# Both partition halves for the low part of the attention keys, and dearer products in the planner's prices

## The chip, the cores and the metric

The kernel runs on one core of a Trainium2 chip. The metric is device time in microseconds (us); three runs of the kernel before gave 3691.1, 3691.89 and 3694.82 us, median 3691.89. A profile of one execution, taken by the hardware profiler, stands beside them. Its engines are called PE (TensorE, matrix products), PEld (TensorE's loads of the stationary operand), DVE (VectorE), ACT (ScalarE), POOL (GpSimd, which here mostly issues transfers) and SP (SyncE, which issues the weight transfers).

## What is computed

Two transformer blocks, of two layers each, on 512 tokens of width 1024, with everything in float32. The parts that this change touches are the attention scores. The first block has neighbourhood attention and context attention in layer 0 (8 heads of 64), and grouped attention over 512 own and 256 context keys in layer 1 (16 query heads, 4 key heads of 64). Each layer of the second block mixes three kinds: latent attention (6 heads of 96), sliding-window attention (6 query heads, 2 key heads of 64) and stick-breaking attention (4 heads of 64).

```
# first block, layer 0 (8 heads, d = 64)
s_loc = einsum(q_r, k_r) * scale          # 256 keys of the window
s_ctx = einsum(q_r, k_ctx) * scale        # 256 context keys
# first block, layer 1 (16 heads on 4 key heads)
s = einsum(qg, k) * dh ** -0.5            # 512 + 256 keys
# second block, per layer
s = einsum(qb, kb) * D ** -0.5            # sliding window, up to 256 keys
z = einsum(qi, k) * scale                 # stick breaking, up to 512 keys, causal
```

Softmax (or the stick-breaking product) and the product with the values follow each; around them stand projections, gated feed-forward layers (width 2816) and norms.

## The kernel before

**Precision.** A float32 operand is split into a high and a low part, each of a type that TensorE takes in one pass. A dense product is then three products into one PSUM bank: high by high, high by low, low by high (`mm3`). Names end in `h` and `l`: `wh`, `wl` for weights, `hnh`, `hnl` for activations.

**Scores of heads of 64.** Here the split is stacked along the contraction. A query tile Q has 128 partitions: the high part of the head in one half of 64, the low part in the other. The key tile K holds the scaled high part of the keys in both halves, so one product of 128 rows gives (high query + low query) by high key. A second product adds high query by low key. The low part of the keys lies only in one half (64 partitions) of its tile (Kl; Klc for context keys, SKl in the second block), so this second product takes the 64 matching partitions of Q as its stationary operand: `q[hs]` by `Kl[hs]`, and a trace shows it as `64*128`, 64 rows by 128 columns. It is called the narrow product, or low product, below. The products of 128 rows show as `128*128`; the latent heads of the second block use three products of 96 rows (`S<-mqkh`, ...). The products with the values, `O<-PTs,...`, are `128*64`, and some of the modulation products `128*32`.

**Making the keys.** `kstack` (line 1560) has two phases. ACT writes the scaled high part to one half of K; then DVE writes the low part to its half of Kl, and ACT copies the high part to K's other half. In layer 0 both heads of a pair share one Kl and one Klc tile. In layer 1 (`g_keys`, line 2025) a pair of key heads shares one Kl, and all four share one Klc. In the second block (`k_item`, line 2416) a pair of stick-breaking heads shares one SKl, while the two sliding-window key heads have one each already (`g_swin`, line 2506).

**Attention pipeline.** `g_pipe` (line 1605) runs items in flight: scores (`qk`, lines 1635, 2080, 2850, 2938) and softmax of one item, transposes of the probabilities two items behind (PT in PSUM, copied by ACT to PTs), products with the values three behind (O). In layer 1 an item is a tile of 128 queries and a head: S<-K,Q and S<-Kl,Q of 512 columns, then Sc<-Kc,Q and Sc<-Klc,Q of 256. Projections of other heads or of the next part fill TensorE in between.

**What sets the order.** The code records its instructions first. A planner (`order`, line 379) then lists them: each engine takes the ready instruction of best priority, with prices in nanoseconds from `price` (line 340), forwards and backwards in four rounds. Tiles come from pools of fixed size: 56 slots of 128x512 (`g`), 8 PSUM banks (`b`), and some for weights. The result is one fixed order for each engine; at run time an engine takes its instructions in that order and waits for what they need. A product of the split type is priced by its columns alone: `max(columns / 2.4, 107) + 2.5`, 215.8 ns for 512 columns. Rows have no price, and a change of shape has none. `warm` (line 571) puts products of a constant with itself (`...<-cons 128x128`) into gaps of 500 ns or more that the plan has on TensorE.

All instructions are written out from one line, L628, so they are told apart by the tiles' names.

Of the kernel before, what the change touches and what calls it, by code (L numbers as in the profile page):

```python
# [165 lines left out]
class _View:  # L166
    """part of a tile; the steps to it are repeated on the real tile"""
# [37 lines left out]
    def box(self):  # L205
        """partitions and columns that bound the view"""
# [34 lines left out]
class _Program:  # L241
    """records instructions, orders them, writes them out"""
# [30 lines left out]
    # ---- recording  # L273
    def glue(self):
        """what is recorded next on one engine stays together"""
        self.glued = _Op()
        o = self.glued
        o.calls, o.pre, o.post, o.tiles, o.cost, o.lag, o.table = [], {}, [], [], 0.0, 0.0, None
# [61 lines left out]
    def price(self, o, name, args, kw, psum):  # L340
        """nanoseconds that an instruction holds its engine"""
        views = [v for v in args if isinstance(v, _View)]
        n = max(v.free() for v in views) if views else 0
        if o.eng == "tensor":
# [10 lines left out]
            else:  # L355
                o.cost += max(b.free() / 2.4, 107.0) + 2.5
# [17 lines left out]
    # ---- ordering  # L374
# [4 lines left out]
    def order(self, prio, seq, window=6000, patience=0.0, margin=0.0, backlog=1e9):  # L379
        """list scheduling: each engine takes the ready instruction of best priority.  # L380

        A tile is only taken if the instructions left can still be run in the order in which
        they stand in seq, with the slots that there are.
        """
# [11 lines left out]
        for t, a in live.items():  # L396
            assert a.max() <= self.caps[t], (t, int(a.max()), int(a.argmax()))
        done = bytearray(N + 1)
# [3 lines left out]
        parked = {t: [] for t in self.caps}  # L402
# [4 lines left out]
        push, pop = heapq.heappush, heapq.heappop  # L407

# [9 lines left out]
        while len(out) < N:  # L418
# [28 lines left out]
            # slots  # L447
            ok = True
            need = {}
            for x in o.tiles:  # L450
# [3 lines left out]
                if a > first and live[x.tag][first:a].max() >= self.caps[x.tag]:  # L454
                    parked[x.tag].append(o)
# [4 lines left out]
                if k > len(s):  # L460
                    parked[x.tag].append(o)
# [9 lines left out]
            for x in o.tiles:  # L471
                if not x.alloc:
# [3 lines left out]
                    if a > first:  # L476
                        live[x.tag][first:a] += 1
            cost = o.cost
# [10 lines left out]
            for x in o.tiles:  # L489
                x.end = max(x.end, o.end)  # L490
                l = x.left
                if len(l) == 1:
                    l.pop()
                    live[x.tag][first:o.k + 1] -= 1
                    push(slots[x.tag], (x.end + 250.0, x.slot))
                else:
# [5 lines left out]
                if parked[x.tag]:  # L502
                    for q in parked[x.tag]:
                        push(avail[q.eng], (q.prio, q.k))
                    parked[x.tag] = []
# [5 lines left out]
            if o.k == first:  # L511
# [5 lines left out]
                for tg in parked:  # L517
                    for q in parked[tg]:
                        push(avail[q.eng], (q.prio, q.k))
                    parked[tg] = []  # L520
# [3 lines left out]
    def mirror(self):  # L524
        """the program from its end to its start"""
# [22 lines left out]
    def schedule(self, rounds=4):  # L548
        """forwards and backwards in turn: what starts late in one direction is urgent in the other"""
# [21 lines left out]
    def warm(self, a, share=0.6, least=500.0):  # L571
        """products of a with itself where the tensor engine would wait: its clock halves when it idles.

        They write to a bank before the tile that comes next in it is started.
        """
# [38 lines left out]
    # ---- writing  # L614
# [16 lines left out]
class _Weights:  # L631
    """stream of weight units: loads run ahead, each unit is split exactly into two float32r parts"""
# [10 lines left out]
    def add(self, key, ap, nk, cols=256, tok=False, g=False):  # L643
        """a unit of nk contraction tiles, in parts: of columns, or (tok) of contraction tiles"""
# [19 lines left out]
    def phases(self, i):  # L664
        """the split of unit i in phases, each to be emitted some time after the one before"""
# [49 lines left out]
    def ahead(self):  # L715
        """the split of the unit after the next, once the matmuls of the present one are out"""
# [7 lines left out]
class _K:  # L724
# [55 lines left out]
    def run_bg(self, budget):  # L780
        """emit background work of about this many microseconds on the vector engine"""
# [20 lines left out]
    def g_rsqrt(self, v, n, out):  # L802
        """v ** -0.5 in small steps that depend on one another; out takes the result"""
# [22 lines left out]
    def sums(self, nt, parts):  # L826
        """sums over the partitions, token-major, of parts that are added one by one"""
# [10 lines left out]
    def stat_p(self, acc):  # L838
        """sums over the partitions, token-major"""
# [6 lines left out]
    def g_stat(self, p, n, out):  # L846
        """one over the root of the mean, from sums of squares"""
# [7 lines left out]
    def stat_b(self, r):  # L855
        """token-major column to a row on all partitions"""
# [6 lines left out]
    def g_row(self, acc, n):  # L863
        """the norm's row, step by step, in a slot of its own"""
# [23 lines left out]
    def apply_items(self, X, rb, A, B, his, los, sl):  # L888
        """scaled and shifted tiles of the normed stream, in two parts"""
# [17 lines left out]
    def update_items(self, X, o, rb, G, acc2, sl, add=None):  # L907
        """residual plus gated, normed branch; squares for the next norm"""
# [42 lines left out]
    def g_postpre(self, X, o, n, acc, G, A, B, his, los, step=256):  # L951
        """post-norm of a branch, residual, pre-norm of the next; one step of tokens after the other"""
# [135 lines left out]
    def load_row(self, i):  # L1088
        """one conditioning vector on all partitions, in two tiles"""
# [9 lines left out]
    def mod_tasks(self, key, rows, outs, bias, blocks):  # L1099
        """background products of conditioning vectors with columns of a modulation matrix"""  # L1100
# [20 lines left out]
    def mods_first(self, q, A, Ac):  # L1121
        """shift and scale of two tiles of features in layer 0, for both streams, on the tensor engine"""
# [25 lines left out]
    def g_mods0(self, r):  # L1148
        """2048 columns of layer 0's modulation for both streams on the tensor engine"""
# [64 lines left out]
    def g_proj_f(self, key, streams, post, step=1.2, k0=0):  # L1214
        """feature-major: weights stationary; post gives the phases after a group"""
# [21 lines left out]
    def g_proj_t(self, key, streams, post, step=1.2):  # L1237
        """token-major: activations stationary"""
# [1938 lines left out]
```

## Time and profile before

| what | before |
|---|---|
| device time, three runs | 3691.1, 3691.89, 3694.82 us |
| span of the profiled execution | 3693.1 us, 1.2 above the median run |
| PE busy | 3667.9 us (99%), 21332 products |
| DVE busy | 2421.1 us (66%) |
| ACT busy | 1601.6 us (43%) |
| POOL busy | 273.0 us (7%) |
| mean granted TensorE clock | 0.988 of full |

The span is the time from the first to the last instruction on the core. The products of a stream overlap, so the end of each is modelled and a busy PE says little about its speed; the distance from one start to the next says how long a product really holds the engine. A chain row follows the last instruction back to whatever released each step.

In order of time the span has: first block layer 0 with its attention (about 100 to 330 us) and two feed-forward layers, layer 1 with its attention (about 1000 to 1260), a feed-forward layer, and the second block's two layers, whose attention lies at about 2100 to 2300 and 3100 to 3310.

### The profile page before, as it was taken

How to read it: one execution, taken by the hardware profiler on the slowest of the kernel's cores; microseconds unless marked ns; L12 is line 12 of the kernel's file. 1: busy time of each engine (PE TensorE's matmuls, PEld its weight loads, DVE VectorE, ACT ScalarE, POOL GpSimd, SP SyncE). 2: the span in 40 equal slices, each digit the busy share in tenths (PEclk: the TensorE clock that was granted, in tenths of full speed). 3: DMA queues.
4: the chain of work that ended last, by engine and by line, in shares of the span. 5: the costliest groups of instructions: out<-in, count | busy, mean ns of one | idle time of the engine just before them, and what ended most of it. 6: DMA issues, size and time to landing. Idle time of an engine off the chain costs nothing.

```text
span 3693.1 us, 55815 instructions
## 1 busy us (share of the span) xinstructions
PE 3667.9 (99%) x21332; PEld 3078.3 (83%) x21332; DVE 2421.1 (66%) x5741; ACT 1601.6 (43%) x2985; POOL 273.0 (7%) x511
## 2 busy tenths in 40 slices
PE   9999999999999999999999999999999999999999
PEld 7689988899976888889888978888888889788887
DVE  4456845699977899998833569994453336694332
ACT  3554533365677643333222458322332235673221
POOL 0110000100001224000000000340000000000000
PEclk9999999999999999998999989999999999899999
DMA  9423322445322558322422322693322232122221
GB/s 319 156 78 132 114 92 97 136 160 184 126 83 101 189 186 288 112 86 76 151 94 84 92 64 90 239 337 103 99 84 97 94 96 77 34 65 97 92 97 63
DMA packets 142908, 458.51 MB, mean 124 GB/s; under 512 B 19872, under 2 KB 21936, under 8 KB 142640
## 3 DMA queue, kind: packets, MB, share of 16 engines
q1 hardware_dynamic: 104400, 331.54, 27.4%
q0 software_dynamic: 38240, 123.41, 9.8%
q8 instruction: 167, 2.74, 0.3%
q14 instruction: 101, 0.83, 0.1%
HBM read 445.43 MB, written 7.34 MB: 123 GB/s over the span
## 4 chain that ended last, share of the span: by engine, by line
PE 97%; DVE 1%; ACT 1%; DMA 0%; issue 0%; SPq 0%; ACTq 0%; DVEq 0%
PE U L628 45%; PE mm L628 32%; PE S L628 5%; PE tl L628 5%; PE O L628 3%; PE PT L628 3%; PE st L628 1%; PE v L628 1%; PE Sc L628 1%; PE mod L628 1%; PE tp L628 1%; PE R L628 0%; PE pq L628 0%; PE rb L628 0%; PE pkv L628 0%
## 5 line engine op out<-in xcount | busy, mean ns | idle before, releaser
L628 ACT ACTIVATE wh<-ws 128x1024 fp32r<-128x1024 f32 (+2 forms) x558 | 571.5, 1027 | 952.5 <-PE mm L628 455.0
L628 DVE TENSOR_TENSOR wl<-ws,wh 128x1024 fp32r<-128x1024 f32 (+2 forms) x558 | 659.9, 1185 | 400.4 <-ACT wh L628 394.9
L628 PE MATMUL U<-hnh,wh 128*128 128x512 f32 (+1 forms) x2048 | 792.5, 387 | 0.0
L628 PE MATMUL U<-hnl,wh 128*128 128x512 f32 (+1 forms) x2048 | 792.3, 387 | 0.0
L628 PE MATMUL U<-hnh,wl 128*128 128x512 f32 (+1 forms) x2048 | 792.0, 387 | 0.0
L628 PEld LDWEIGHTS U<-hnh,wl 128*128 128x128 f32 x2048 | 384.6, 188 | 84.5
L628 PEld LDWEIGHTS U<-hnl,wh 128*128 128x128 f32 x2048 | 384.6, 188 | 84.5 <-DVE hnl L628 0.2
L628 PEld LDWEIGHTS U<-hnh,wh 128*128 128x128 f32 x2048 | 384.5, 188 | 84.4
L628 PE MATMUL mm<-hdh,wl 128*128 128x512 f32 x960 | 378.3, 394 | 0.0
L628 PE MATMUL mm<-hdh,wh 128*128 128x512 f32 x960 | 378.2, 394 | 0.0
L628 PE MATMUL mm<-hdl,wh 128*128 128x512 f32 x960 | 377.9, 394 | 0.0
L628 DVE SCALAR_TENSOR_TENSOR wm<-wm,crow 128x512 f32<-128x512 f32 x384 | 249.8, 687 | 0.1
L628 DVE SCALAR_TENSOR_TENSOR cv<-U,vecs,cv 128x511 f32<-128x511 f32 (+1 forms) x264 | 173.2, 659 | 85.6 <-ACT cv L628 81.6
L628 PEld LDWEIGHTS mm<-hdl,wh 128*128 128x128 f32 x960 | 180.3, 188 | 42.4
L628 PEld LDWEIGHTS mm<-hdh,wl 128*128 128x128 f32 x960 | 180.2, 188 | 42.3
L628 PEld LDWEIGHTS mm<-hdh,wh 128*128 128x128 f32 x960 | 180.3, 188 | 42.0
L628 DVE TENSOR_TENSOR sg<-sg,U 128x512 f32<-128x512 f32 x88 | 60.6, 688 | 204.6 <-PE U L628 195.0
L628 ACT ACTIVATE cv<-U,vecs 128x512 f32<-128x512 f32 (+1 forms) x132 | 93.0, 706 | 224.0 <-PE U L628 224.0
L628 POOL DMA_DIRECT2D wm<-in_w_mod x288 | 154.3, 537 | 330.2 <-DVE wm L628 88.4
L628 PE MATMUL mm<-wh,hnh 128*128 128x256 f32 (+1 forms) x576 | 169.3, 294 | 0.0
L628 ACT ACTIVATE sg<-U 128x512 f32<-128x512 f32 x88 | 52.3, 594 | 256.9 <-PE U L628 256.9
L628 PE MATMUL mm<-wl,hnh 128*128 128x256 f32 (+1 forms) x576 | 162.4, 282 | 0.2 <-DVE wl L628 0.2
(505 smaller groups left out, 7160.4 us busy)
## 6 DMA issues: line engine op xcount, KB each, us to landing
ws<-in_w_gu SPq DMA_DIRECT2D x176, 512.0 KB, 3.8
wm<-in_w_mod POOLq DMA_DIRECT2D x288, 256.0 KB, 5.0
ws<-in_w_up SPq DMA_DIRECT2D x132, 512.0 KB, 4.0
ws<-in_w_da SPq DMA_DIRECT2D x64, 512.0 KB, 3.7
wm<-in_w_ada POOLq DMA_DIRECT2D x96, 256.0 KB, 3.4
ws<-in_w_dna SPq DMA_DIRECT2D x48, 512.0 KB, 3.8
ws<-in_w_in SPq DMA_DIRECT2D x44, 512.0 KB, 4.6
wa<-in_w_ada SPq DMA_DIRECT2D x64, 256.0 KB, 6.3
```

The costliest lines, as they stand in the source:

```text
L628: getattr(getattr(tc.nc, o.eng), name)(*[real(v) for v in args], **{k: real(v) for k, v in kw.items()})
```

## The change

The low part of the keys is kept on both halves of its tile. `kstack` gets one more DVE instruction, which copies the low part to the other 64 partitions. Every head then has a Kl (and its own columns of a Klc, or its own SKl), and all low products take the whole query tile: `q` by `Kl`, 128 rows. That product is (high query + low query) by low key, so low by low is now included as well.

In the planner, a product's price becomes `max(columns / 2.25, 103) + 4`: 231.6 ns for 512 columns, 117.8 for 256 (109.2 before), 107 for 128 (109.5 before). The search for free slots is written with other bookkeeping (`full`, `behind`, `noslot` in place of `parked`). Docstrings and comments are gone, so all instructions now come from line 651.

```diff
@@ price
-                o.cost += max(b.free() / 2.4, 107.0) + 2.5
+                o.cost += max(b.free() / 2.25, 103.0) + 4.0
@@ order
-                if a > first and live[x.tag][first:a].max() >= self.caps[x.tag]:
-                    parked[x.tag].append(o)
+                if a > full[x.tag]:
+                    push(behind[x.tag], (a, o.k))
...
@@ kstack
-            nc.vector.scalar_tensor_tensor(kl[lo or hs], p[hs], 0.125, k_[hs].bitcast(F32), ALU.mult, ALU.subtract)
+            nc.vector.scalar_tensor_tensor(kl[hs], p[hs], 0.125, k_[hs].bitcast(F32), ALU.mult, ALU.subtract)
             nc.scalar.activation(k_[os_], k_[hs].bitcast(F32), AF.Copy)
+            nc.vector.tensor_copy(kl[os_], kl[hs].bitcast(F32))
@@ g_qk, layer 0
-            Kl = self.g("Kl", F32R)
+            Kl = [self.g("Kl", F32R) for _ in range(2)]
...
@@ g_attn0, qk
+            Kcl = Klc[:, h * TC:(h + 1) * TC]
...
-                    nc.tensor.matmul(o, q[hs], Klc[hs, :TC], start=False, stop=True)
+                    nc.tensor.matmul(o, q, Kcl, start=False, stop=True)
...
-            nc.tensor.matmul(S3, q[hs], loc(Kl[hs]), start=False, stop=True)
+            nc.tensor.matmul(S3, q, loc(Kl[h]), start=False, stop=True)
...
@@ layer 1, g_keys and qk
-                kl_ = self.g("Kl", F32R)
+                kl_ = [self.g("Kl", F32R) for _ in range(2)]
+                klc_ = self.g("Klc", F32R)
...
-            nc.tensor.matmul(S, q[hs], Kl[kv][hs], start=False, stop=True)
+            nc.tensor.matmul(S, q, Kl[kv], start=False, stop=True)
             nc.tensor.matmul(c, q, Kc[kv], start=True, stop=False)
-            nc.tensor.matmul(c, q[hs], Klc[kv][hs], start=False, stop=True)
+            nc.tensor.matmul(c, q, Klc[kv], start=False, stop=True)
@@ second block
-                ph.append(self.kstack(SK[-1], kl, p, h))
+                SKl.append(self.g("SKl", F32R))
+                ph.append(self.kstack(SK[-1], SKl[-1], p, h))
...
-                nc.tensor.matmul(S[:, cs], q[:64], Kl[e][:64, k0:k0 + n], start=False, stop=True)
+                nc.tensor.matmul(S[:, cs], q, Kl[e][:, k0:k0 + n], start=False, stop=True)
...
-            nc.tensor.matmul(S[:, :n], q[hs], Kl[h][hs, :n], start=False, stop=False)
+            nc.tensor.matmul(S[:, :n], q, Kl[h][:, :n], start=False, stop=False)
```

The number of products stays: 288 low products before and after. DVE gets 36 more instructions (they show as CAST), one for each call of `kstack`: 24 of 64x512 and 12 of 64x256. ACT, POOL and SP have as many instructions as before. The order changes on every engine. Three places follow, of the program before and of the changed one.

The first is TensorE in layer 1's attention, some way into the stage. S and Sc are the scores of own and of context keys, with K, Kc the high and Kl, Klc the low keys; PT are transposes and O the products with the values. Before:

```order
L628 MATMUL S<-K,Q 128x512
L628 MATMUL S<-Kl,Q 128x512
L628 MATMUL PT<-cons,E 128x128
L628 MATMUL Sc<-Kc,Q 128x256
L628 MATMUL Sc<-Klc,Q 128x256
L628 MATMUL O<-PTs,V 64x128 x8
```

Now:

```order
L651 MATMUL S<-K,Q 128x512
L651 MATMUL S<-Kl,Q 128x512
L651 MATMUL PT<-cons,E 128x128 x3
L651 MATMUL Sc<-Kc,Q 128x256
L651 MATMUL Sc<-Klc,Q 128x256
L651 MATMUL PT<-cons,E 128x128
L651 MATMUL O<-PTs,V 64x128 x4
```

The sizes are those of the output, which don't tell the 64 rows before from the 128 now. High and low products still stand in turn; transposes moved between a low product and O, and O is taken in smaller groups.

The second is TensorE where the sliding-window scores of the second block's first layer begin. SK, SKl and SQ are keys, low keys and queries, tp are transposes. Before:

```order
L628 MATMUL tp<-cons,qs 128x128 x7
L628 MATMUL O<-PTs,vsb 64x128 x8
L628 MATMUL tp<-cons,mq 96x128 x4
L628 MATMUL S<-SK,SQ 128x128
L628 MATMUL S<-SKl,SQ 128x128
```

Now:

```order
L651 MATMUL O<-PTs,vsb 64x128 x8
L651 MATMUL tp<-cons,mq 96x128 x8
L651 MATMUL S<-cons 128x128 x3
L651 MATMUL S<-SK,SQ 128x128
L651 MATMUL S<-SK,SQ 128x256
L651 MATMUL S<-SKl,SQ 128x128
```

Four more transposes of mq were drawn ahead of the scores, and three products of the constant with itself were put into a gap.

The third is DVE at the same place, where the low keys SKl and the queries SQ are made; E is the first instruction of the softmax, and ra, rb, ry are steps of a root that another part needs. Before:

```order
L628 SCALAR_TENSOR_TENSOR SQ<-tp,vecs,SQ 64x512
L628 SCALAR_TENSOR_TENSOR ry<-rb,ry 128x16
L628 SCALAR_TENSOR_TENSOR SKl<-kg,SK 64x512 x2
L628 SCALAR_TENSOR_TENSOR SQ<-tp,vecs,SQ 64x512
L628 TENSOR_TENSOR ra<-ry 128x16
L628 SCALAR_TENSOR_TENSOR SQ<-tp,vecs,SQ 64x512
L628 ISA E,ms<-S,swb 128x128
```

Now:

```order
L651 SCALAR_TENSOR_TENSOR rb<-ra,msv 128x16
L651 SCALAR_TENSOR_TENSOR SQ<-tp,vecs,SQ 64x512
L651 SCALAR_TENSOR_TENSOR SKl<-kg,SK 64x512 x2
L651 CAST SKl<-SKl 64x512 x2
L651 SCALAR_TENSOR_TENSOR SQ<-tp,vecs,SQ 64x512 x2
L651 ISA E,ms<-S,swb 128x128
```

The two copies stand between the low keys and the last two query tiles ahead of the softmax; one small step of the root went elsewhere.

## Rows read from the trace of the kernel before

**Rows 1.** The chain that ended last, its shares of the span by engine and tile.

```profile
by line: PE U L628 44.6%; PE mm L628 31.8%; PE S L628 4.7%; PE tl L628 4.6%; PE O L628 3.0%; PE PT L628 2.9%; PE st L628 1.1%; PE v L628 1.0%; PE Sc L628 1.0%; PE mod L628 0.6%; PE tp L628 0.5%; PE R L628 0.4%; PE pq L628 0.4%; PE rb L628 0
```

**Rows 2.** Products grouped by shape: count | busy us, mean ns | idle before.

```profile
L628 PE MATMUL U<-hnl,wh 128*128 128x512 f32 x1920 | 756.1, 394 | 0.0
...
L628 PE MATMUL S<-Kl,Q 64*128 64x512 f32 x64 | 31.8, 497 | 0.0
...
L628 PE MATMUL S<-mqkh,mqkl 96*128 96x512 f32 x12 | 4.7, 396 | 0.0
```

**Rows 3.** All narrow products, by tile: count, duration ns (min/median/max), first and last start.

```profile
L628 PE MATMUL S<-SKl,SQ x80: 322/440/579, 2111.5 to 3224.8; 64*128 64x256 f32 x44, 64*128 64x128 f32 x20, 64*128 64x384 f32 x8, 64*128 64x512 f32 x8
...
L628 PE MATMUL S<-Kl,Q x96: 381/492/502, 108.1 to 1242.7; 64*128 64x512 f32 x64, 64*128 64x256 f32 x32
...
L628 PE MATMUL Sc<-Klc,Q x64: 276/381/391, 1027.2 to 1241.3; 64*128 64x256 f32 x64
...
L628 PE MATMUL S<-Klc,Q x32: 378/382/386, 115.3 to 262.0; 64*128 64x256 f32 x32
...
L628 PE MATMUL S<-Klc,Qc x16: 378/381/386, 117.2 to 233.7; 64*128 64x256 f32 x16
```

**Rows 4.** TensorE in time order, layer 1 attention: start us, duration us, product.

```profile
1184.46 0.38 PE L628 MATMUL Sc<-Kc,Q 128*128 128x256 f32 x1
1184.78 0.38 PE L628 MATMUL Sc<-Klc,Q 64*128 64x256 f32 x1
1185.09 0.38 PE L628 MATMUL Sc<-Kc,Q 128*128 128x256 f32 x1
```

**Rows 5.** The weight load of the last product of rows 4.

```profile
1185.09 0.19 PEld L628 LDWEIGHTS Sc<-Kc,Q 128*128 128x128 f32 x1
```

**Rows 6.** TensorE in time order, streams of one shape: 256 columns, then 512.

```profile
1251.39 0.28 PE L628 MATMUL tl<-ych,wl 128*128 128x256 f32 x1
1251.51 0.28 PE L628 MATMUL tl<-ych,wh 128*128 128x256 f32 x1
...
2010.40 0.39 PE L628 MATMUL U<-hnl,wh 128*128 128x512 f32 x1
2010.63 0.40 PE L628 MATMUL U<-hnh,wl 128*128 128x512 f32 x1
```

**Rows 7.** TensorE in time order, sliding-window scores of the second block's first layer.

```profile
2195.49 0.44 PE L628 MATMUL S<-SK,SQ 128*128 128x128 f32 x1 [1.45 <-DVE SQ L628]
...
2204.29 0.58 PE L628 MATMUL S<-SKl,SQ 64*128 64x256 f32 x1
2204.80 0.58 PE L628 MATMUL S<-SK,SQ 128*128 128x256 f32 x1
...
2208.88 1.09 PE L628 MATMUL tp<-cons,mq 128*96 128x128 f32 x4
```

**Rows 8.** By stretch: its us, busy us (instructions) of PE, PEld, DVE, ACT, POOL; clock, DMA.

```profile
100.00:330.00 230.00, 229.37 (x1543) 178.32 (x1541) 135.30 (x428) 126.93 (x272) 32.42 (x62) 1.00 0.38 123
1040.00:1240.00 200.00, 199.78 (x1472) 139.40 (x1469) 147.81 (x438) 151.45 (x387) 31.04 (x58) 1.00 0.28 93
...
2190.00:2222.00 32.00, 28.70 (x118) 18.25 (x117) 20.76 (x111) 20.94 (x66) 1.74 (x4) 0.63 0.07 20
...
3185.00:3222.00 37.00, 33.60 (x129) 22.82 (x131) 23.14 (x128) 22.05 (x70) 0.00 (x0) 0.58 0.00 1
```

**Rows 9.** DVE in time order, same sliding-window stretch: idle time in brackets.

```profile
2203.89 0.29 DVE L628 CUSTOM_DVE_ANT_0 E<-S,swb 128x128 f32<-128x128 f32 x1 [4.17 <-PE S L628]
```

**Rows 10.** DVE groups by shape: copies, and the weight split.

```profile
L628 DVE COPY rw<-l 128x128 f32<-128x128 f32 x72 | 16.0, 223 | 0.7
...
L628 DVE COPY PTs<-PT 128x512 f32<-128x512 f32 x4 | 2.7, 686 | 0.0
...
L628 DVE TENSOR_TENSOR wl<-ws,wh 128x1024 fp32r<-128x1024 f32 x480 | 585.6, 1222 | 360.4 <-ACT wh L628 354.9
```

More of the change, by code (lines that the diff above doesn't have):

```diff
@@ L397, in order, with full_from @@
             assert a.max() <= self.caps[t], (t, int(a.max()), int(a.argmax()))
+        def full_from(t, k):
+            l, c = live[t], self.caps[t]
+            while k <= N:
+                e = min(k + 512, N + 2)
+                hit = l[k:e] >= c
+                i = int(hit.argmax())
+                if hit[i]:
+                    return k + i
+                k = e
+            return N + 2
+        full = {t: full_from(t, 0) for t in self.caps}
         done = bytearray(N + 1)
@@ L401, in order @@
         avail = {e: [] for e in self.ENG}
-        parked = {t: [] for t in self.caps}
+        noslot = {t: [] for t in self.caps}
+        behind = {t: [] for t in self.caps}
         far = []
@@ L407, in order, with freed @@
         push, pop = heapq.heappush, heapq.heappop
+        def freed(t):
+            h = behind[t]
+            while h and h[0][0] <= full[t]:
+                q = ops[pop(h)[1]]
+                push(avail[q.eng], (q.prio, q.k))
         def enter(o):
@@ L460, in order @@
                 if k > len(s):
-                    parked[x.tag].append(o)
+                    noslot[x.tag].append(o)
                     ok = False
@@ L477, in order @@
                         live[x.tag][first:a] += 1
+                        full[x.tag] = min(full[x.tag], full_from(x.tag, first))
             cost = o.cost
@@ L495, in order @@
                     push(slots[x.tag], (x.end + 250.0, x.slot))
+                    for q in noslot[x.tag]:
+                        push(avail[q.eng], (q.prio, q.k))
+                    noslot[x.tag] = []
                 else:
@@ L501, in order @@
                     live[x.tag][l[-1] + 1:b + 1] -= 1
[L502 to L505, printed above, removed]
+                full[x.tag] = full_from(x.tag, full[x.tag])
+                freed(x.tag)
             for q in o.post:
@@ L516, in order @@
                     push(pend[q.eng], (q.ready, q.prio, q.k))
[L517 to L520, printed above, removed]
+                for tg in full:
+                    if full[tg] < first:
+                        full[tg] = full_from(tg, first)
+                        freed(tg)
         self.out = out
@@ L1397, in post @@
                     elif si == 0:
-                        ph.append(self.kstack(K[h], Kl, p, h))
+                        ph.append(self.kstack(K[h], Kl[h], p, h))
                     else:
-                        ph.append(self.kstack(Kc[:, h * TC:(h + 1) * TC], Klc[:, :TC], p, h))
+                        ph.append(self.kstack(Kc[:, h * TC:(h + 1) * TC], Klc[:, h * TC:(h + 1) * TC], p, h))
                 return [lambda a=a, b=b: (a(), b()) for a, b in zip(*ph)]
@@ L1558, in layer0, with kstack @@
         return (xh, xl, T), (ch, cl, TC), tail
-    def kstack(self, k_, kl, p, h, lo=None):
+    def kstack(self, k_, kl, p, h):
         nc = self.nc
@@ L1636, in qk @@
             n, h = items[i]
-            hs = slice(64 * h, 64 * h + 64)
             S = self.mm("S")
             st[i] = S
+            Kcl = Klc[:, h * TC:(h + 1) * TC]
             if n == "c":
@@ L1651, in qk @@
             nc.tensor.matmul(S3, q, loc(K[h]), start=True, stop=False)
-            nc.tensor.matmul(S3, q[hs], loc(Kl[hs]), start=False, stop=True)
+            nc.tensor.matmul(S3, q, loc(Kl[h]), start=False, stop=True)
             nc.tensor.matmul(S[:, 256:], q, Kc[:, h * TC:(h + 1) * TC], start=True, stop=False)
-            nc.tensor.matmul(S[:, 256:], q[hs], Klc[hs, :TC], start=False, stop=True)
+            nc.tensor.matmul(S[:, 256:], q, Kcl, start=False, stop=True)
         def soft(i):
@@ L2022, in layer1 @@
         K, Kc, Kl, Klc = [], [], [], []
-        klc = self.g("Klc", F32R)
         def g_keys():
@@ L2033, in g_keys @@
                     Kc.append(kc_[:, h * TC:(h + 1) * TC])
-                    Kl.append(kl_)
-                    Klc.append(klc[:, pr * TC:(pr + 1) * TC])
+                    Kl.append(kl_[h])
+                    Klc.append(klc_[:, h * TC:(h + 1) * TC])
                 ps = []
@@ L2082, in qk @@
             kv = pair // 2
-            hs = slice(64 * (kv % 2), 64 * (kv % 2) + 64)
             if h == 0:
@@ L2417, in k_item @@
             p = fps[1][c]
-            kl = self.g("SKl", F32R)
             ph = []
@@ L2421, in k_item @@
                 SK.append(self.g("SK", F32R))
-                SKl.append(kl)
-                ph.append(self.kstack(SK[-1], kl, p, h))
+                SKl.append(self.g("SKl", F32R))
+                ph.append(self.kstack(SK[-1], SKl[-1], p, h))
             return [lambda: (ph[0][0](), ph[1][0]()), lambda: (ph[0][1](), ph[1][1]())]
@@ L2544, in item @@
                     kg = self.g("kg")
-                    ks = [self.kstack(SKs[h], SKls[h], kg, h, slice(0, 64)) for h in range(2)]
+                    ks = [self.kstack(SKs[h], SKls[h], kg, h) for h in range(2)]
                     return [a, lambda: nc.scalar.activation(kg, p[0], AF.Copy, scale=self.vec("swa_k", l, 1)),
@@ L2940, in qk @@
             h = 2 * pr + hh
-            hs = slice(64 * hh, 64 * hh + 64)
             n = (t + 1) * P
```

## The prediction

> **What bounds the kernel now.** I read the page first: PE is busy 99% of the span. That share proves little, since overlapping products always look busy, so the chain comes next. By line it is nearly all PE: the dense products U and mm lead, while the scores S and Sc hold 4.7% and 1.0% of it [rows 1]. TensorE is the bound, inside the attention stages too, so whatever shortens its own stream there shortens the span until another engine is as late.
>
> Then I looked for products that cost more than their columns. Grouped by shape, a product of 512 columns lasts 394 ns with 128 rows and 396 ns with 96, but 497 ns as a narrow one of 64 rows [rows 2]. Durations overlap, so the price is read from the starts. In layer 1 high and low products of 256 columns stand in turn, and starts are 0.32 and 0.31 us apart [rows 4]; in a stream of one shape 256 columns take 0.12 us and 512 take 0.23 [rows 6]. Each change between 128 and 64 rows therefore costs about 0.195 us, in both directions. The weight load tells how: it starts together with its product, at 1185.09 [rows 5, 4], so it wasn't done ahead. A product of 96 rows pays nothing of the kind [rows 2].
>
> Last I looked at how near the other engines are. In layer 0's attention DVE is busy 135 of 230 us and ACT 127; in layer 1's steady part DVE 148 and ACT 151 of 200 [rows 8].
>
> **The change, part by part.**
>
> *Switches removed.* There are 80 + 96 + 64 + 32 + 16 = 288 narrow products [rows 3], and nearly each has a switch before and one behind. Counted over the whole written order, neighbours on TensorE differ in shape (narrow, `128*64`, `128*32`, or full) 906 times before. With the low products full this falls to 374, since the switches to O and to the modulation products stay, and a low product next to O still meets one. So 532 go: 532 x 0.195 = 104 us. The chain gives a second estimate: S and Sc hold 5.7% of 3693.1 = 210 us. Their columns at the stream's rate are 144 products of 512 (33 us), 376 of 256 (45), 16 of 384 and 40 of 128 (some 7), and the latent products and masks (some 27), together about 112. The rest, 98 us, agrees, and part of the cost falls on the product behind. Bounds: 98 and 112 (288 x 2 x 0.195); I take 104.
>
> *At half clock.* In the sliding-window scores starts are 0.51 us apart [rows 7] in a stretch whose granted clock averages 0.63 (0.58 in the second layer's) [rows 8], that is, mostly the lower level, 1.2 of 2.4 GHz, after TensorE had waited 1.45 us and shortly before [rows 7]. 256 columns at 1.2 GHz take 0.21, so a switch costs 0.30 there, 0.1 more than counted. With 28 products in that block by the written order, and the like in the second layer: -6 us. Bounds: 0 and, if the clock also holds, -11.
>
> *What comes back in layer 1.* Some 45 of the 104 us lie in this stage. Its steady 200 us would shrink to about 158, against 151 of ACT and 148 of DVE, which is 96% and 94%: three engines level, each waiting on the others through eight PSUM banks. If ACT gets to 90%, the stretch takes 168: +10. Bounds: 0, and +31 if ACT reaches only 80% (189 us; it is at 76% now). I take 10, since ACT and DVE have waited for S and PT here rather than the other way round, and part of DVE's work in this stage, the modulation vectors, can move into later stages.
>
> *What comes back at the sliding window.* The block runs from 2195.49 to 2208.88 [rows 7], 13.4 us, and would take 3.4 to 6. DVE waited 4.17 us for these scores [rows 9] and once more as long behind them, so it can follow by about 8 us; beyond that the softmax is late next: +2 a layer, +4. Bounds: 0 and +16 (no gain there at all).
>
> *Copies added.* 36 on DVE. The trace has no copy of 64 partitions from SBUF. The nearest rows are 0.223 us for 128 columns and 0.686 for 512, the latter out of PSUM [rows 10]; per copy that is the range, 8 to 25 us of DVE in all. I take 0.45, near the middle, as the source is SBUF and the size the larger one. In layers 0 and 1 they lie beside other products, in DVE's idle time: there only the first keys can be late, and the planner has projections to run meanwhile; without that cover it is 0.45 a pair, 2 us. At the sliding window two copies stand ahead of the last queries, and TensorE does wait for DVE's SQ [rows 7]. Behind them queue the SQ and the first softmax: 0.9 us a layer, +2. Bounds: 0 and +5. That wait of 1.45 us itself stays.
>
> *Planner.* Dearer products and the other slot bookkeeping reorder every engine but add no instruction, no transfer, and two constant products fewer. Three more tiles of 56 are held through layer 1, two through stick breaking; what yields is the early fetching of modulation matrices, due later. I take 0, with bounds of 12 either way: one stretch at half clock more or less. (The one at 2190 is about 24 us long, from a mean of 0.63 over 32 us, so half of 24.) The 64 more rows of each product I cost at nothing: in rows 2 products of 96 and of 128 rows last the same.
>
> **A rule that speaks against it.** A stream of full products hides its weight loads: 0.12 us for 256 columns is no more than what the columns need [rows 6]. The Trainium skill, page "TensorE: Matmul & The Clock Gate", section "Part 3: Packing small matmuls — row/col tiling", says that a weight load overlaps products in flight only when its row group differs. By that rule the low product, now on the same rows as the high one, would still wait for its load, and the gain would be about nothing; by rows 6 it is the 104. The trace disagrees with the rule for full tiles, so I keep the 104.
>
> **Sum.** Against the execution's own span: 3693.1 - 104 - 6 + 10 + 4 + 2 + 0 = 3599. The span is 1.2 us above the median of the runs shown, so the forecast is 3598 us.
>
> **Rivals.**
>
> *The other engines take over.* ACT gets no further than 80% in layer 1 (+31 in place of +10), the sliding window gives nothing (+16 in place of +4) and the copies cost 5: 3598 + 21 + 12 + 3 = 3634. For it: three levels within 6% in rows 8. Against: layer 0 and stick breaking have room, and ACT and DVE wait for PE now.
>
> *The clock holds as well.* The plan has three constant products ahead of the first sliding-window scores, and the denser scores keep TensorE busier. Then layer 1 loses nothing (-10), the half-clock block gains 11 in place of 6, and the rest of the two slow stretches, some 10 us each, runs in half: 3598 - 10 - 5 - 10 = 3573. Against: TensorE still waits there for DVE.
>
> *The rows aren't the cause.* If the wait came from the change of operands (by that page's rule, for instance), all 532 stay: 3692 + 2 = 3694. Rows 2 and 6 speak against it: the 96-row and dense products change operands each time.
>
> *Slower.* In the feed-forward layers the planner now believes that a 512 product takes 231.6 ns rather than 215.8, so for 48 products of a unit it can leave a weight split (wl, 1.22 us, rows 10) 0.76 us later. If the split then comes late by that much in each unit, TensorE waits; from 124 units on (94 / 0.76; 480 splits of this size [rows 10], two a unit, make 240) the gain is gone, and with all of them late the time is 3598 + 182 = 3780. Against: 231.6 is what rows 6 show, so a plan with it has true slack.
>
> **How the numbers follow.** Forecast 0.62 (its own range 3580 to 3616), other engines 0.17, clock 0.15, rows not the cause 0.03, slower 0.03. The range for 8 in 10 goes from 3570, the clock case, to 3636, the other-engines case. A measurement of this kernel tells about 0.2% (7 us) from no change. The first three cases are all faster by more: 0.94; same 0.03, slower 0.03.
>
> **What would show it.** Right: S<-Kl of 512 columns at about 394 ns in the groups by shape, starts 0.12 and 0.23 us apart in the layer 1 stretch, the stage some 35 us shorter, layer 0's by 25 to 30, the second block's by 15 each; CAST rows of 0.3 to 0.6 us; ACT near 90% in layer 1. Wrong: starts still 0.3 apart (rows not the cause); full-rate products with idle time before them that ends with ACT or DVE in layer 1 (other engines); a feed-forward layer in which products wait for wl (slower).

## Result: 3594.85 us, against a forecast of 3598

Four runs of the changed kernel gave 3593.6 to 3596.7 us, median 3594.85; the kernel before, run beside it, had a median of 3693.36. The ratio is 0.9732, 95% interval 0.9718 to 0.9746: about 98.5 us less. The profiled execution spans 3591.8 us, 101.3 less than the one before.

From here on a stage is measured from the last product of the feed-forward layer ahead of it (in layer 0 the span's start, in layer 1 its first projection) to the first product U behind it (products of the constant that are named U count as U in the second block and not in layer 1, where they would move the gain by 2 us). Its changes of shape are counted over TensorE's products as the trace has them: neighbours that differ as 64 rows, 64 or 32 columns, or full.

| stage | before, us | after, us | gain | changes of shape | at 0.195 each |
|---|---|---|---|---|---|
| first block, layer 0 | 401.1 | 375.3 | 25.8 | 268 to 117 | 29.4 |
| first block, layer 1 | 348.1 | 311.6 | 36.5 | 373 to 134 | 46.6 |
| second block, layer 0 | 222.6 | 206.8 | 15.8 | 130 to 58 | 14.0 |
| second block, layer 1 | 227.5 | 204.1 | 23.4 | 136 to 66 | 13.7 |
| all the rest | | | -0.2 | | |

The stretches between these stages, mostly feed-forward layers, kept their length to 1.6 us each, and the differences cancel. All of the gain lies where the scores are.

### The profile page after: what moved, and what is told of

Its sections match the earlier page's. It is cut to its first block, busy times and chain, and to the rows that moved or that the text cites. A ratio compares the mean times of both kernels' runs of the same rounds, so it can differ in the third digit from the quotient of the medians.

```text
span 3591.8 us, 55858 instructions
## 1 busy us (share of the span) xinstructions
PE 3558.8 (99%) x21328; PEld 3047.7 (85%) x21328; DVE 2419.0 (67%) x5777; ACT 1595.3 (44%) x2985; POOL 273.5 (8%) x511
## 3 DMA queue, kind: packets, MB, share of 16 engines
q0 software_dynamic: 38240, 123.41, 10.1%
## 4 chain that ended last, share of the span: by engine, by line
PE 91%; DVE 7%; ACT 1%; issue 1%; DMA 0%; ACTq 0%; DVEq 0%; SPq 0%; POOLq 0%
PE U L651 44%; PE mm L651 31%; PE tl L651 3%; PE O L651 3%; PE S L651 3%; PE PT L651 3%; PE v L651 1%; DVE t5o L651 1%; DVE wl L651 1%; PE mod L651 1%; PE st L651 1%; DVE X L651 1%; PE tp L651 1%; DVE u L651 1%; PE Sc L651 0%
```

## The profile after

The chain by line answers to [rows 1]: S fell from 4.7% of the span to 2.5%, Sc is gone from what the row shows, and VectorE's lines (t5o, wl, X) have come up, at 1% or less each.

```profile
by line: PE U L651 44.4%; PE mm L651 30.5%; PE tl L651 3.0%; PE O L651 2.9%; PE S L651 2.5%; PE PT L651 2.5%; PE v L651 1.0%; DVE t5o L651 1.0%; DVE wl L651 1.0%; PE mod L651 0.9%; PE st L651 0.9%; issue 0.7%; DVE X L651 0.6%; PE tp L651 0.
```

The products by shape answer to [rows 2]: the low product of 512 columns shows as `128*128` and lasts 401 ns, not 497, near a dense product's 393.

```profile
L651 PE MATMUL U<-hnl,wh 128*128 128x512 f32 x1920 | 755.4, 393 | 0.0
...
L651 PE MATMUL S<-Kl,Q 128*128 128x512 f32 x64 | 25.6, 401 | 0.0
```

TensorE in time order in layer 1's attention answers to [rows 4]. Starts of 256 columns are 0.11 or 0.12 us apart, where they were 0.32 and 0.31; of 512 columns, 0.24.

```profile
1123.56 0.40 PE L651 MATMUL S<-Kl,Q 128*128 128x512 f32 x1
1123.80 0.28 PE L651 MATMUL Sc<-Kc,Q 128*128 128x256 f32 x1
1123.91 0.28 PE L651 MATMUL Sc<-Klc,Q 128*128 128x256 f32 x1
1124.03 0.28 PE L651 MATMUL Sc<-Kc,Q 128*128 128x256 f32 x1
```

The weight loads of the same products answer to [rows 5]. The load of Sc<-Klc starts at 1123.80, with the product ahead of its own, and runs beside it, 0.11 us ahead of its own product.

```profile
1123.80 0.19 PEld L651 LDWEIGHTS Sc<-Klc,Q 128*128 128x128 f32 x1
```

So a low product on the same 128 rows as its neighbour doesn't wait for its load. The Trainium skill's rule in "TensorE: Matmul & The Clock Gate", section "Part 3: Packing small matmuls — row/col tiling" (a load overlaps only when its row group differs) would have kept the starts at 0.3; this trace disagrees with it.

The sliding-window scores of the second block's first layer, TensorE in time order, answer to [rows 7]. The stretch is still at the lower level of the clock, but 256 columns now take 0.21 us, not 0.51.

```profile
2126.65 0.50 PE L651 MATMUL S<-SK,SQ 128*128 128x128 f32 x2 [1.05 <-ACT SK L651]
...
2129.70 0.45 PE L651 MATMUL S<-SK,SQ 128*128 128x128 f32 x1 [1.11 <-DVE SQ L651]
...
2131.33 0.41 PE L651 MATMUL S<-SKl,SQ 128*128 128x256 f32 x1
2131.54 0.41 PE L651 MATMUL S<-SK,SQ 128*128 128x256 f32 x1
...
2135.42 0.53 PE L651 MATMUL PT<-cons,E 128*128 128x128 f32 x2
```

The block runs from 2126.65 to 2135.42: 32 score products in 8.8 us, with waits of 0.47 and 1.11 us for DVE among them, where 28 took 13.4.

Four stretches answer to [rows 8], with the same columns: layer 0's attention, layer 1's steady part, and the two sliding windows.

```profile
74.00:304.00 230.00, 226.83 (x1680) 186.30 (x1679) 139.96 (x430) 135.14 (x281) 41.79 (x80) 0.99 0.47 154
1011.00:1211.00 200.00, 199.65 (x1822) 168.63 (x1821) 177.36 (x545) 169.60 (x442) 43.41 (x81) 1.00 0.41 134
2122.00:2154.00 32.00, 27.50 (x218) 22.62 (x218) 30.38 (x167) 30.49 (x96) 5.17 (x10) 0.89 0.32 104
3098.00:3135.00 37.00, 33.25 (x265) 28.17 (x264) 35.73 (x203) 36.25 (x117) 0.00 (x0) 0.91 0.01 2
```

Two things stand in them. At the sliding windows DVE and ACT are busy 30.4 and 30.5 of 32 us (20.8 and 20.9 before): with TensorE waiting for DVE's SQ and ACT's SK just above, they are the bound there now. And a mean clock of 0.89 over 32 us is 0.11 x 2 x 32 = 7 us at the lower level, of 0.91 over 37 also 7; before, by 0.63 and 0.58, it was 24 and 31.

DVE's copies, by shape, and its wait inside the sliding-window block, which answers to [rows 9]: 0.41 us where it was 4.17.

```profile
L651 DVE CAST Kl<-Kl 64x512 fp32r<-64x512 f32 x12 | 5.1, 422 | 0.3
...
L651 DVE CAST SKl<-SKl 64x512 fp32r<-64x512 f32 x12 | 5.1, 422 | 0.4
L651 DVE CAST Klc<-Klc 64x256 fp32r<-64x256 f32 x12 | 3.5, 288 | 0.3
```

```profile
2133.38 0.29 DVE L651 CUSTOM_DVE_ANT_0 E<-S,swb 128x128 f32<-128x128 f32 x1 [0.41 <-PE S L651]
```

New against the kernel before are three waits of TensorE near the start of layer 0's attention, 3.0 us together.

```profile
123.33 1.07 PE L651 MATMUL PT<-cons,E 128*128 128x128 f32 x8 [1.07 <-ACT E L651]
125.33 1.30 PE L651 MATMUL PT<-cons,E 128*128 128x128 f32 x5 [0.93 <-DVE rw L651]
131.11 0.63 PE L651 MATMUL PT<-cons,E 128*128 128x128 f32 x4 [1.04 <-ACT PTs L651]
```

## The experiments

### Rows alone, price alone

Three kernels take the change apart. The first is the kernel before with the new price, the second the changed kernel with the old price:

```diff
-                o.cost += max(b.free() / 2.4, 107.0) + 2.5
+                o.cost += max(b.free() / 2.25, 103.0) + 4.0
```

> The kernel before with only the planner's new price for a matmul; the low products still read 64 rows. Theory (the time is the switches between 128-row and 64-row products, and the price is worth nothing): some 902 changes of shape on TensorE against 907, so 5 x 0.195 = -1 us: 3693, between 3685 and 3701. Rival (the better price lets the planner order the work better and gave part of the 98 us): 3660 to 3680, with the feed-forward stages shorter as well.

> The changed kernel with the planner's old price for a matmul: all score products use 128 rows, the copies are there. Theory (rows alone carry the gain): 366 changes of shape against 375, 3595, between 3587 and 3603. Rival (the price gave part of it): 3615 to 3635, the rest of the way back to 3693 being what the price gave.

The third keeps the changed kernel's order and copies, and cuts the operands of every low product back to 64 rows when it is written out, which comes to this, here and at the other low products:

```diff
-            nc.tensor.matmul(S, q, Kl[kv], start=False, stop=True)
+            nc.tensor.matmul(S, q[hs], Kl[kv][hs], start=False, stop=True)
```

> The changed kernel, with the same order on every engine and the same copies, but each low product reads only the 64 matching rows again, as in the kernel before. Theory (a price per change of shape of a product): 923 changes against 375, 548 x 0.195 = +107, so about 3700, between 3685 and 3710; of that some 26 us by the end of layer 0's attention and some 37 more in layer 1's. Rival (order, copies or the planner's new plan gave the gain): 3595 to 3610.

Measured: price alone 3683.36 us (3680.52 to 3687.26; ratio 0.9973, 0.9962 to 0.9984); rows with the old price 3597.14 (0.9740, 0.9725 to 0.9755); narrow products in the new order 3691.10 (0.9998, 0.9988 to 1.0007). The second and third lie within their ranges. With every instruction in the same place the 64 rows cost 3691.1 - 3594.85 = 96.3 us. The rows are the cause, and the trace of the third kernel has the old spacing again:

```profile
1150.56 0.39 PE L655 MATMUL Sc<-Kc,Q 128*128 128x256 f32 x1
1150.88 0.38 PE L655 MATMUL Sc<-Klc,Q 64*128 64x256 f32 x1
1151.19 0.50 PE L655 MATMUL S<-K,Q 128*128 128x512 f32 x1
```

That is 923 against 375 changes, 548 for 96.3 us, or 0.176 each: by stage 27.7 us for 154 in layer 0 (0.18), 38.3 for 237 in layer 1 (0.16), 31.9 for 157 in the second block (0.20); the profiled stages add up to 97.9. Against the kernel before, the narrow kernel in the new order is 2.4 us shorter, so order, copies and price together are worth no more than that.

The first kernel missed its expected range (3685 to 3701) by 2 us at the near side. Its trace says where the 10 us came from: the first three stages stand within 4 us (layer 1 is 3.5 longer), the stretches between the stages are 3.6 us shorter in all, and the last stage takes 216.0 us in place of 227.5. There its sliding window has a mean clock of 0.77 (17 us at the lower level) where [rows 8] has 0.58 (31 us):

```profile
3185.00:3222.00 37.00, 36.47 (x201) 25.13 (x201) 27.61 (x170) 28.23 (x97) 0.00 (x0) 0.77 0.01 1
```

So another order there is worth some 10 us to the narrow kernel, while in the changed kernel the new price gives 2.3 us, within the spread of the runs.

### Copies twice

```diff
             nc.vector.tensor_copy(kl[os_], kl[hs].bitcast(F32))
+            nc.vector.tensor_copy(kl[os_], kl[hs].bitcast(F32))
```

> The changed kernel with each of its 36 copies of a low part issued twice on VectorE. Theory (the copies lie beside TensorE's work except at the sliding windows): +2 us, 3595 to 3600. Rival (the copies are on the path): 36 times the duration of a copy, by the estimate of 0.45 us each +16, 3611.

Measured: 3595.34 us (3593.78 to 3600.0), 0.5 above the changed kernel, within the spread. The added copies are 24 x 0.42 + 12 x 0.29 = 13.6 us of DVE; nearly nothing of it reaches the span. The planner drew up a new order for this kernel, so a cost of 2 or 3 us at the sliding windows isn't excluded: in its profile the second block's layers are 0.7 and 2.1 us longer, and other stretches shorter.

### A price per change, or per narrow product?

The kernel before, with the products of layer 1's items, and of the two heads' items in layer 0, written in another order (layer 1's is shown):

```diff
             nc.tensor.matmul(S, q, K[kv], start=True, stop=False)
-            nc.tensor.matmul(S, q[hs], Kl[kv][hs], start=False, stop=True)
             nc.tensor.matmul(c, q, Kc[kv], start=True, stop=False)
+            nc.tensor.matmul(S, q[hs], Kl[kv][hs], start=False, stop=True)
             nc.tensor.matmul(c, q[hs], Klc[kv][hs], start=False, stop=True)
```

> The kernel before (low products on 64 rows), with the score and context products of an item written out so that low products stand next to each other: 738 changes of shape on TensorE instead of 907, the number of low products unchanged. Theory (a price per change of shape): 169 x 0.195 = -33 us, 3660, between 3645 and 3672 (the lower end if paired low products of the two heads in layer 0, which lie on different row halves, also run side by side: their starts would then be some 0.01 us apart); layer 0's attention some 13 us shorter, layer 1's some 20. Rival (a price per narrow product, whatever stands before it): 3693.

Measured: 3658.82 us (3658.32 to 3659.91; ratio 0.9906, 0.9889 to 0.9922): 34.8 us for 169 changes fewer, with all 288 narrow products still there. Layer 0 got 11.9 shorter, layer 1 18.9, the second block 0.4 in its first layer and 1.8 in its second. A price per narrow product would have left the time at 3693: the price is per change. That the sum came so close is in part luck, since the stages don't follow their counts alone: 63 changes fewer in layer 0, 119 in layer 1 (0.16 each), 13 more in the second block. TensorE in layer 1, time order, shows how it falls:

```profile
1121.40 0.50 PE L628 MATMUL S<-K,Q 128*128 128x512 f32 x1
1121.75 0.28 PE L628 MATMUL Sc<-Kc,Q 128*128 128x256 f32 x1
1121.95 0.50 PE L628 MATMUL S<-Kl,Q 64*128 64x512 f32 x1
1122.29 0.28 PE L628 MATMUL Sc<-Klc,Q 64*128 64x256 f32 x1
```

Between two high products (behind one of another shape) 512 columns take 0.35, 0.12 over; the 256 columns ahead of the change take 0.20, 0.08 over; the 512 behind it 0.34, 0.11 over. In the medians over this trace a full product ahead of a change is 0.09 late and the one behind it 0.106: together the 0.195 of the forecast, but on two products. And in layer 0 the two heads' low products, on different halves, pass as one: two take 0.32 us (191.22 to 191.54), a single one 0.31 (186.45 to 186.76). There are 33 such pairs, their starts 0.003 us apart, so some 4 of layer 0's 11.9 us are columns that now run side by side (33 x 0.12) and not changes saved.

```profile
186.45 0.38 PE L628 MATMUL S<-Klc,Qc 64*128 64x256 f32 x1
186.76 0.50 PE L628 MATMUL mm<-hnh,wh 128*128 128x512 f32 x1
...
191.22 0.39 PE L628 MATMUL S<-Kl,Q 64*128 64x256 f32 x2
191.54 0.51 PE L628 MATMUL S<-Kc,Q 128*128 128x256 f32 x2
```

### The changes that are left

Of the 375 changes that the changed kernel still has, most are at the products O (64 columns). Two kernels go after them: O in runs of up to 12 products in place of 4, and, with that, a charge in the planner for a change of columns.

```diff
-... len(self.ops[-1].calls) < 4:
+... len(self.ops[-1].calls) < 12:
@@ second kernel, order
+                if shape is not None and s_ != shape:
+                    cost += 195.0
```

> The changed kernel, with the products of the probabilities and values (64 columns wide) kept together up to 12 in a row instead of 4: 290 changes of shape on TensorE against 375. Theory (the same price for a change to a product that uses 64 columns of the array): 85 x 0.195 = -17 us, 3578, between 3570 and 3588. Rival (a product with fewer columns pays nothing for the change, only one with fewer rows): 3595. Rival 2 (holding the products back delays what waits for them): 3597 to 3610.

> As the previous one, and the planner also charges 195 ns to a product whose number of columns of the array differs from the one before it: 274 changes of shape against 375. Theory: 101 x 0.195 = -20 us, 3575, between 3565 and 3588. Rivals as for the previous one: 3595 if columns cost nothing, above it if the order that the charge gives makes something late.

Measured: 3596.11 (3594.95 to 3597.41) and 3595.97 us (3594.19 to 3597.84): no gain, and my forecast of -17 and -20 failed. The price wasn't the fault. The changed kernel first, then the one with longer runs; the trace records an O product twice, so 8 and 24 records are 4 and 12 products:

```profile
1122.57 0.66 PE L651 MATMUL O<-PTs,V 128*64 128x128 f32 x8
1123.16 0.33 PE L651 MATMUL R<-cons,rw 128*128 128x128 f32 x1
```

```profile
1040.79 1.53 PE L651 MATMUL O<-PTs,V 128*64 128x128 f32 x24
1042.25 0.33 PE L651 MATMUL R<-cons,rw 128*128 128x128 f32 x1
```

From the run's first start to the next product, 8 records take 0.59 us and 24 take 1.46: 0.0545 for each record, and 0.15 over for each run. To that come 0.094 on a product of 128 columns ahead of the run (0.203 us, where a stream has 0.109), and 0.056 to 0.106 on the full product behind it. A run costs 0.30 to 0.35 us, each of its two changes 0.15 to 0.18, little less than a change of rows.

In layer 1 the runs of O went from 67 to 31, and what the intervals at them take beyond their columns at the stream's rate from 21.7 to 10.2 us, 11.5 saved. Nearly all of it came back as later starts elsewhere in the stage: the intervals between full products have 25.7 us beyond their columns, where they had 15.0, and the stage stayed at 311.1 us (in the second kernel it is 315.2, and layer 0 is 4.0 shorter). That is rival 2's mechanism, just short of its range; rival 1, that such a change is free, is wrong.

### Who holds layer 1 after the change

ScalarE's exponentials of layer 1 no longer sum their rows, in the changed kernel and in the one with the longer runs of O:

```diff
-                    E, st[i - 1 + h][0], AF.Exp, scale=rq[:, h:h + 1], bias=m[:, h:h + 1], accum_out=l[:, h:h + 1])
+                    E, st[i - 1 + h][0], AF.Exp, scale=rq[:, h:h + 1], bias=m[:, h:h + 1])
```

> The changed kernel, with ScalarE's work in layer 1's attention made shorter: its 128 exponentials no longer sum their rows, which takes away 128 instructions of 0.234 us, 30 us of ScalarE in that stage (the denominators are taken from the maxima instead). Theory (after the change TensorE still bounds layer 1, ScalarE at 91% is only near it): the stage, 311.6 us, gets 0 to 6 shorter, 3589 to 3597. Rival (ScalarE took over there and holds back 10 us or more): stage about 300, 3583 or less.

> The same relief of ScalarE together with the products of probabilities and values kept together up to 12 in a row, which alone took 15 us of changes of shape off TensorE in layer 1 and gave all of it back as waits. Theory (what gave it back is ScalarE and VectorE being nearly as busy as TensorE): with the relief the 15 us come through at least in half: the stage 297 to 304 us, the whole 3580 to 3589. Rival (the longer groups themselves hold back the transposes and what waits for them): stage about 311, 3594 to 3598.

Measured: 3587.60 us (3584.19 to 3591.64) and 3583.55 (3578.42 to 3584.94). The whole stage as one stretch, columns as in [rows 8], first the changed kernel:

```profile
935.80:1247.40 311.60, 306.84 (x2667) 272.07 (x2665) 286.71 (x889) 232.74 (x569) 57.80 (x108) 0.98 0.42 137
```

The longer runs of O:

```profile
936.20:1247.30 311.10, 302.40 (x2670) 274.84 (x2669) 288.12 (x894) 233.53 (x571) 58.20 (x109) 0.98 0.41 140
```

The relief alone:

```profile
937.90:1248.00 310.10, 304.64 (x2654) 270.41 (x2653) 292.26 (x889) 225.50 (x443) 56.16 (x105) 0.99 0.42 139
```

Both:

```profile
932.80:1233.50 300.70, 293.82 (x2650) 269.55 (x2649) 278.46 (x849) 221.99 (x441) 52.06 (x98) 0.99 0.40 133
```

The relief alone shortens the stage by 1.5 us. It was smaller than worked out, though: the 128 instructions overlap the exponentials, and ACT's busy time in the stage fell by 7.2 us (232.7 to 225.5), not by 30. So the kernel shows that ACT isn't what holds the stage by 10 us, and little more; VectorE, busy 287 of 311.6 us in the changed kernel, wasn't relieved. That TensorE bounds the stage still has a better witness in the changed kernel's own trace: there TensorE stands waiting for other engines for 4.1 us of it. (The whole is 7 us shorter, under its expected range by 1.4; most of that lies in the second block, which the edit doesn't touch, so it is another order's doing.)

The longer runs alone: 0.5. Both: 10.9, as forecast. There the intervals at O have 8.9 us beyond their columns in place of 21.7, and only 3.7 of the 12.8 came back. What let it through isn't shown: ACT is busy 10.7 us less than in the changed kernel, but DVE 8.2 less too, with 40 instructions fewer within the stage, and the planner drew up a new order. No kernel here that computes the whole beats the changed one.

### Narrow products at the sliding window alone

The changed kernel, with only these low products cut back, when they are written out:

```diff
-                nc.tensor.matmul(S[:, cs], q, Kl[e][:, k0:k0 + n], start=False, stop=True)
+                nc.tensor.matmul(S[:, cs], q[:64], Kl[e][:64, k0:k0 + n], start=False, stop=True)
```

> The changed kernel, with the same order and copies, but the 48 low products of the sliding-window scores (24 a layer) read only 64 rows again. Theory 1 (a change of shape costs its 0.195 and nothing hangs on the clock): 96 x 0.195 = +19, 3614, with half-clock stretches of some 7 us there as in the changed kernel. Theory 2 (the narrow products also lengthen the half-clock stretch, and cost 0.1 more in it): stretches of 20 us and more again, +24 to +32, 3619 to 3627.

Measured: 3616.46 us (3612.6 to 3618.91), +21.6, between the two theories. The two stages are 11.1 and 10.2 us longer for 94 changes (18.3 at 0.195). The lower clock is back, by 0.63 and 0.77 for 24 and 17 us, and with it the 0.51 spacing:

```profile
2135.14 0.58 PE L655 MATMUL S<-SK,SQ 128*128 128x256 f32 x1
2135.65 0.58 PE L655 MATMUL S<-SKl,SQ 64*128 64x256 f32 x1
```

```profile
2127.00:2159.00 32.00, 29.28 (x119) 19.11 (x116) 22.48 (x112) 21.47 (x67) 1.62 (x3) 0.63 0.12 40
3118.00:3155.00 37.00, 35.85 (x194) 24.27 (x195) 27.02 (x165) 27.13 (x95) 0.00 (x0) 0.77 0.00 1
```

So theory 2 was right in what it said of the clock, and its price was too high: beyond the 18.3 the longer stretch costs 3 us, no more than the spread of the runs. The lengths at the lower level are clearer than their worth: in one profile each, the five kernels with narrow scores here have 17 to 31 us of it at each sliding window, the seven with full ones 3 to 14.

## Why the prediction came out right

*Switches removed (-104): the mechanism right, the term some 6 too large.* 532 changes went, as counted. With the order held still, 548 cost 96.3 us net of all that comes back, 0.176 each. Their own price is a little more. The narrow kernel in the new order and the changed kernel have the same products in the same sequence, so intervals can be set side by side: 0.09 ahead of a change and 0.104 behind it, but 0.056 where the product behind has 128 columns, as behind 125 of the 288 low products. That adds up to 101 us for 548, 0.184 each, or 98 for 532. Some full scores in the changed kernel seem 0.08 to 0.09 us late as well, but that is no loss: each follows a product of 128 columns that shows as little too short (at 1105.11 and 1105.13, 0.03 and 0.20 us for 128 and 256 columns, 0.23 together, as in a stream). That products of 96 rows pay nothing was read from durations, which can't tell; the starts bear it out, 0.121 us for 256 columns and 0.235 for 512 ahead of a product of 128 rows.

*Half clock (-6) and what comes back at the sliding window (+4): net -2 forecast, about -3 found* (21.3 less 18.3, in the last experiment; -4 by the side-by-side sum). The price of a change at the lower level was right: 0.51 - 0.21 = 0.30. The block took 8.8 us, where 3.4 to 6 had been worked out for TensorE and about 8 for DVE, which it waits for, as that step said. What it didn't have is the clock: the stretches at the lower level went from 24 and 31 us to 7 each, as in the rival "the clock holds as well". That came in, but its worth is within those 3 or 4 us rather than the 15 of that rival.

*What comes back in layer 1 (+10): the mechanism right, about half of the amount, and the rest luck.* 46.6 at 0.195 less the measured 36.5 is 10.1, but three things make it up. Against the narrow kernel in the same order 46.2 less 38.3 is 7.9. Of that 2.4 is the price again (49 low products with 128 columns behind them), and 5.5 are intervals that grew: 4 of them between 980 and 1040 us, where the attention starts and TensorE waits for ACT's E and DVE's rot, up to 1.2 us at a time. The other 2.2 are the new order's. So the waits that were forecast took some 5 us, mostly at the start of the stage and not in its steady part, where ACT is at 85% and DVE at 89%, not the 90% of ACT that I looked for.

*Layer 0 (no return forecast): 25.8 of 29.4.* Against the narrow kernel in the same order it is 27.7 of 30.0; 1.2 of the difference is the price behind 128 columns, 1.1 came back. The three waits shown above aren't due to quicker scores: the narrow kernel in the new order has them too, and in that order it is 2.0 us slower here than the kernel before.

```profile
127.71 1.06 PE L655 MATMUL PT<-cons,E 128*128 128x128 f32 x8 [1.12 <-ACT E L655]
129.70 0.74 PE L655 MATMUL PT<-cons,E 128*128 128x128 f32 x5 [0.93 <-DVE rw L655]
...
134.05 0.63 PE L655 MATMUL PT<-cons,E 128*128 128x128 f32 x4 [1.04 <-DVE l L655]
```

*Copies (+2): 0.5 by doubling them, within the spread;* their 0.42 us was put at 0.45.

*Planner (0, within 12): right for the sum.* Old price against new is 2.3 us, and everything but the rows 2.4. By stage the new order does more: the narrow kernel in it is 2.0 and 1.8 us slower in the first block's layers, 0.6 and 6.7 faster in the second's. That is why the last stage gained 23.4 and not the 15 that I looked for; in the same order it gains 16.8.

So what was found adds up to -98 for the changes, +5.5 and +1.1 given back, -4 at the sliding windows and -2.4 for order, copies and price together: -97, against 98.5 measured and 94 forecast. The first term was some 6 us too large; the returns in layers 0 and 1, the sliding windows, and copies and planner erred the other way by 3.4, 2 and 4.4. That they cancel so well is luck. (The range's upper end, 3636, should have been 3634 by the rival's own sum.)

*Rivals.* "The rows aren't the cause" fell with the narrow kernel in the same order, "slower" with the feed-forward layers, which stayed as long as they were. "The other engines take over" didn't happen at this size of gain, but the kernel with longer runs of O shows that a further saving on TensorE comes back.

## What to carry to other kernels

Count the changes of a product's shape in the order that TensorE runs, and read their price from the distance between starts, with a stream of one shape beside it; durations of overlapping products hide it. If the operand can be made full at the price of a few copies on an engine with room, or the products of one shape be put together, the time comes back without any product less. And before a second gain of the same kind is counted in, look whether the engines behind have room left: the longer runs of O took 11.5 us off TensorE's changes and gave 0.5; together with a small relief elsewhere, and another order, 10.9 came through.

## What the runs showed of the hardware

A change between 128 and 64 rows costs 0.09 us on the product ahead and 0.106 behind (0.056 if that one has 128 columns). A change to or from 64 columns costs little less, 0.15 to 0.18 us: 0.094 on a 128-column product ahead of the run, 0.15 within the run, 0.056 to 0.106 on the product behind. Two products of 64 rows on different halves of the rows, one behind the other, take the time of one (0.32 against 0.31 us). And narrow products keep TensorE longer at the lower clock: with the same work and order, 24 and 17 us against 7 and 7.
